# Loading a ranked expert's gate and up matrix in one 2 MB transfer instead of two of 1 MB

## The chip, the cores and the metric

The kernel runs on one core of a Trainium2 chip. The metric is the device time of one execution in microseconds, the median of the runs. The core's engines work side by side, each through its own list of instructions: TensorE (PE) multiplies, VectorE (DVE), ScalarE (ACT) and GpSimd (POOL) do the rest, and SyncE (SP) issues nearly all transfers from memory (HBM) to the on-chip memory (SBUF). Semaphores hold an instruction until what it needs is there.

## The reference

One layer of a decoder trunk for 256 tokens of width 1024 in float32: an adaptive norm, a mixer (convolution module and differential attention, gated and summed), and a second adaptive norm with a mixture of 64 small experts, of which each token uses 8, and a shared expert. The change lies in the experts:

```python
g, u = jnp.split(jnp.einsum('td,edf->tef', tc, w_gu), 2, axis=-1)
return jnp.einsum('tef,efd->td', jax.nn.silu(g) * u * gc[..., None], w_down)
```

`w_gu` of one expert is 1024 x 512 (2 MB) and `w_down` 256 x 1024 (1 MB), so the experts bring 192 MB of weights through the core's transfers.

## The kernel before

**Blocks.** After routing, the kernel orders the experts by how many tokens chose them, and packs their tokens into blocks of 128 rows. Blocks 0 to 2 hold six experts known beforehand (numbers 0 to 5), blocks 3 to 27 the 58 ranked ones. The string `PAT` (L36) gives the kinds of blocks 3 to 27: `Q` packs four experts of 32 rows, `P` two of 64, `M` one of 96 and one of 32, `H` one of 128. The numbers of the experts of a kind run on, so block 3 (Q) holds 44 to 47, block 4 (P) 14 and 15, block 5 (Q) 48 to 51, block 6 (Q) 52 to 55, block 7 (P) 16 and 17, block 8 (Q) 56 to 59, block 9 (P) 18 and 19, block 10 (P) 20 and 21; block 25 (Q) holds 60 to 63, block 26 (P) 34 and 35, block 27 (P) 36 and 37.

**Work of one block on PE** (`experts`, L1799): the gate and up product, eight k steps with one matmul for each expert in every step (L1811, called GU below); the combination of the block before (L1719); two transposes (L1836); half the gather of a later pair of blocks (L1528) and two small steps (L1569, L1572); the down product (L1862, called D). Then the next block's GU. The last block's down product is `finale` (L1744, L1756). The shared expert's matmuls (L1793, L1634, L1656) are put between them.

**Weights.** They come through one list of loads in a fixed order, L306 to L346: for a block, the first half of the gate and up matrix (k steps 0 to 3) of each of its experts, then the second halves, then the down matrices. Each load is 1 MB and goes to a landing place of 8 KB in each of the 128 partitions. From block 3 on 14 places are handed out again and again, named by their offset in KB: 0, 8, 16, 24, 32, 40, 96, 104, 112, 120, 128 and 136 in the tile `fa`, 144 and 152 in `late_w`. `advance` (L361) gives the next load of the list the place that has been free longest, and `load` (L384) issues it with `dma` (L269) on SP's queue. `done` (L435) frees a place: a first half's when GU has done k step 3, a second half's after k step 7, a down matrix's after D. In blocks 0 and 1 a place is handed on by halves (`halves`, L359): after two k steps its first half takes half of the next load, 512 KB. SP waits for the place's last reader before it issues a transfer, and also for the transfer eight before it, since eight semaphores are used in turn.

**Order.** A planner (`Plan`, L49) runs while the program is built: every piece of work is a coroutine with an estimated cost, and the planner's clock decides in which order the instructions are written and which place each load gets. At run time that order is fixed.

Of the kernel before, what the change touches and what calls it, by code (L numbers as in the profile page):

```python
# [18 lines left out]
KB = 256  # L19
# [20 lines left out]
class Event:  # L40
    t = None
# [159 lines left out]
def tile_hybrid_block(ctx, tc, x, c, positions, w_ada, b_ada, norm1_g, w_in, conv_dw, conv_dw_b,  # L201
# [21 lines left out]
    late_w = []  # L223
    B = [ps.tile([P, 512], F32, name=f"bank{i}") for i in range(8)]

    def fa(kb, n):
        return FA[:, int(kb * KB):int(kb * KB) + n]
# [41 lines left out]
    def dma(o, i):  # L269
        return nc.sync.dma_start(o, i)  # L270
# [51 lines left out]
    blocks = [("P", [i, i + 1]) for i in range(0, NS, 2)]  # L322
    for kd in pat:
        js = []
# [14 lines left out]
    for b in [1, 0, 2, *range(3, len(blocks))]:  # L339
        js = blocks[b][1]  # L340
        gs = [("g", j, q) for q in range(2) for j in js]
        ds = [("d", j, 0) for j in js]
        if b == len(blocks) - 1:
            ds = [("d", j, 0, cs) for cs in ENDS for j in js]
            gs = [("g", j, q, c_) for q in range(2) for c_ in range(2) for j in js]
        order += gs + ds  # L346
# [3 lines left out]
    loaded = {}  # L350
    todo = list(order)
    eid, idi = {}, []
# [5 lines left out]
    halves, LAST = {}, 160  # L358
    w2s = ExitStack()  # L359

    def advance(now, half=None):  # L361
        pool = pl.pools["w"]
        while todo:
            kind, i, q, *cut = todo[0]
            more = cut and cut[0] in (1, *ENDS[1:])
            if not pool and not more and half is None:
                return
            w = loaded.setdefault((kind, i), Weights())
            if kind in ("g", "d") and i >= NS and not idi:
                return  # L370
            todo.pop(0)
            if not more:
                pool.sort(key=lambda e: e[0])
                w.slot, off = pool.pop(0) if half is None else (now, half)
                if not q:
                    w.k, w.at, w.off = [None] * 16, [0.0] * 16, []
                w.off.append(off)
            if half is not None:
                halves[half] = kind, i, q
                load(kind, i, q, [0], now)  # L380
                return
            load(kind, i, q, cut, now)

    def load(kind, i, q, cut, now):  # L384
        w = loaded[kind, i]
        off = w.off[q]
        if kind in ("g", "d"):
            wsrc = w_exp_gu if kind == "g" else w_exp_down
            if i < NS:
                wsrc = wsrc[0, i]  # L390
            else:
                if i not in eid:
                    eid[i] = nc.sync.value_load(idi[0][0:1, i:i + 1], min_val=0, max_val=NE - 1)
                wsrc = wsrc[0, bass.ds(eid[i], 1)].rearrange("o a b -> (o a) b")
        elif kind in ("sg", "sd"):
            wsrc = (w_sh_gu if kind == "sg" else w_sh_down)[0]
        elif kind == "b":
            wsrc = w_ada[0][:, q * D + i * 256:q * D + (i + 1) * 256]
        else:
            wsrc = src[kind][i]  # L400
        nk = {"d": 2, "sd": 2, "b": 8}.get(kind, 4)
        t = fa(off, 2048) if off < 144 else late_w[0][:, (off - 144) * KB:(off - 136) * KB] if off < LAST else late_w[1]
        t = t.rearrange("p (k n) -> p k n", k=nk)
        wsrc = wsrc.rearrange("(p k) n -> p k n" if kind in ("g", "d", "sg", "sd") else "(k p) n -> p k n", p=P)
        if kind != "b":
            wsrc = wsrc[:, q * nk:(q + 1) * nk]
        cuts = 2 if cut else 1
        st = max(dma_free[0], max(w.slot, now) + 2.0)
        size = (2.48 if kind in ("g", "d", "sg", "sd") else 2.92) / max(cuts, 1)
        if cut and cut[0] in ENDS:  # L410
            dma(t[:, :, cut[0]], wsrc[:, :, cut[0]])
            st += 2.48 * (cut[0].stop - cut[0].start) / D
            w.k[0:2] = t[:, 0], t[:, 1]
            pl.ev("Ld", i, cut[0].start).t = 0.0
            w.ends = {**getattr(w, "ends", {}), cut[0].start: st + ARRIVE}
            cut = []
            cuts = 0
        for c_ in cut or range(cuts):
            ks = slice(c_ * nk // cuts, (c_ + 1) * nk // cuts)
            dma(t[:, ks], wsrc[:, ks])  # L420
            st += size
            for k in range(ks.start, ks.stop):
                w.at[q * nk + k] = st + ARRIVE
                w.k[q * nk + k] = t[:, k]
                pl.ev("L", kind, i, (q * nk + k) // 2).t = 0.0
        dma_free[0] = st
        if q and params and kind != "b" and not cut and cuts:
            n, prm = params.pop(0)
            dma(*prm)
            pl.ev("param", n).t = st + ARRIVE  # L430

    def done(key, q, now=None):
        now = pl.cur.ready if now is None else now
        w = loaded[key]
        if w.off[q] in halves:  # L435
            e = halves.pop(w.off[q])
            load(*e, [1], now)
            advance(now)
        elif w.off[q] in once:
            once.remove(w.off[q])  # L440
        elif w.off[q] == LAST:
            w2s.close()
            obs = ctx.enter_context(tc.tile_pool(name="obs", bufs=1)).tile([P, 8 * KB], F32R, name="obs")
            pl.put("ob", *(ob_of(obs[:, i * D:(i + 1) * D]) for i in range(2)))
        else:
            pl.pools["w"].append((now, w.off[q]))
            advance(now)

    advance(0.0)


# [887 lines left out]
    key = late([NE, NE + 1])  # L1339
# [624 lines left out]
    with tc.If(novf > 0):  # L1964
        wg = fa(0, 4096).rearrange("p (k n) -> p k n", k=K)
        wd = fa(16, 2 * D).rearrange("p (k n) -> p k n", k=2)
        gcol, sg, act, aT = fa(88, 2), fa(89, 256), fa(90, 256), fa(91, 256).rearrange("p (f s) -> p f s", f=2)
        with tc.For_i(0, novf, 1) as i:
# [5 lines left out]
            for t in range(2):  # L1974
# [9 lines left out]
                for h in range(2):  # L1984
                    d = slice(h * 512, (h + 1) * 512)
# [31 lines left out]
```

## Time and profile before

| | us |
|---|---|
| median of 3 runs (820.06 to 821.34) | 820.31 |
| the profiled execution | 821.83 |
| its span in the trace | 820.0 |
| PE busy in the span | 768.2 (94%) |
| DVE, ACT, POOL busy | 444.6, 325.5, 192.0 |

The transfers moved 271 MB, of which 192 MB are the experts'. The page's strip has 40 slices of 20.5 us, and a digit is the busy share in tenths; for the transfers it is the mean share of 16 DMA engines. The timeline lists one engine's instructions, neighbours of a kind merged: start, length, line, count, and in brackets the idle time ahead of it and what ended that. A float32 matmul stands there as two instructions, so the GU of a P block is x32, that of a Q block x64. Where experts' places lie in two tiles, the rows of one k step are split in two.

### The profile page before, as it was taken

The numbers are of one execution on the slowest core, as the hardware profiler recorded it, in microseconds if no ns is written. First come the engines' busy times: TensorE is split into PE (matmuls) and PEld (weight loads), VectorE is DVE, ScalarE is ACT, GpSimd is POOL, SyncE is SP. The second block draws the span as 40 slices with busy tenths as digits, with TensorE's granted clock in tenths as the row PEclk, the third lists the DMA queues.
The fourth block names the chain that finished last, engine by engine and source line by source line (L and its number), as shares of the span: only waits on it lengthen the run. The fifth ranks groups of instructions, "written<-read, shape, count | busy, mean of one in ns | idle before, by whom it ended". The sixth has DMA issues, their size and how long they took to land.

```text
span 820.0 us, 13174 instructions
## 1 busy us (share of the span) xinstructions
PE 768.2 (94%) x4759; PEld 473.9 (58%) x4759; DVE 444.6 (54%) x1035; ACT 325.5 (40%) x714; POOL 192.0 (23%) x246
## 2 busy tenths in 40 slices
PE   3999999899996999999999697899999999999997
PEld 2898777589793987745454152354464455454543
DVE  5458988979996677543433041344344344433343
ACT  4357656864758864323222021233232232232220
POOL 3003888778573683100001000000000000000000
PEclk9999989889998999999999899999999999999999
DMA  9998766537554586389999999999999999999993
GB/s 319 364 344 279 263 248 219 194 116 256 206 194 166 179 302 231 133 328 362 404 420 420 422 421 420 420 422 421 420 421 420 421 422 420 420 421 418 419 412 132
DMA packets 69883, 271.04 MB, mean 331 GB/s; under 512 B 6085, under 2 KB 15893, under 8 KB 46520
## 3 DMA queue, kind: packets, MB, share of 16 engines
q1 hardware_dynamic: 69464, 270.00, 84.4%
q8 instruction: 38, 0.62, 0.3%
q0 software_dynamic: 304, 0.16, 0.1%
q14 instruction: 29, 0.24, 0.1%
q10 hardware_dynamic: 48, 0.01, 0.0%
HBM read 269.11 MB, written 1.05 MB: 329 GB/s over the span
## 4 chain that ended last, share of the span: by engine, by line


## 5 line engine op out<-in xcount | busy, mean ns | idle before, releaser
L1811 PE MATMUL bank<-fa 128*32 128x512 f32 (+2 forms) x1048 | 203.1, 600 | 11.3 <-DMA fa<-in_w_exp_gu_dram 11.3
L1811 PEld LDWEIGHTS bank<-fa 128*32 128x32 f32 (+2 forms) x1048 | 60.9, 123 | 133.3 <-issue 108.0
L863 DVE SCALAR_TENSOR_TENSOR bank<-fa,tap,bank 128x256 f32<-128x256 f32 x232 | 113.0, 487 | 6.1
L1685 DVE SCALAR_TENSOR_TENSOR fa<-bank,gsc,h 128x256 f32<-128x256 f32 x28 | 13.6, 484 | 170.9 <-ACT h L1681 170.9
L1862 PE MATMUL bank<-fa 128*32 128x512 f32 (+1 forms) x496 | 84.9, 596 | 0.8 <-DMA fa<-in_w_exp_down_dram 0.7
L1681 ACT ACTIVATE h<-bank 128x256 f32<-128x256 f32 x28 | 10.8, 385 | 187.9 <-PE bank L1811 187.9
L776 POOL TENSOR_TENSOR rb<-fa,rb 128x512 fp32r<-128x512 f32 x46 | 60.1, 1314 | 65.8 <-ACT rb L795 63.9
L1703 DVE TENSOR_TENSOR fa<-bank,fa 128x512 f32<-128x512 f32 x54 | 37.4, 692 | 65.2 <-PE bank L1862 65.0
L776 POOL TENSOR_TENSOR ra<-fa,ra 128x512 fp32r<-128x512 f32 x48 | 63.8, 1335 | 25.6 <-ACT ra L795 22.2
L1728 DVE TENSOR_TENSOR fa<-fa,bank 128x512 f32<-128x512 f32 x108 | 66.9, 681 | 0.0
L1771 ACT CAST obs<-fa 128x512 fp32r<-128x512 f32 x54 | 33.4, 619 | 82.6 <-DVE fa L1703 82.6
L795 ACT CAST ra<-fa 128x512 fp32r<-128x512 f32 x76 | 46.8, 622 | 40.9 <-PE bank L812 24.6
L1528 PE MATMUL bank<-ra 128*128 128x256 f32 x448 | 60.7, 288 | 0.0
L1496 ACT ACTIVATE fa<-bank,b2c,a2c 128x256 f32<-128x256 f32 x108 | 53.6, 561 | 17.7 <-PE bank L1528 16.7
L1719 PE MATMUL bank<-obs,ra 128*128 128x512 f32 x216 | 58.9, 413 | 0.0
L795 ACT CAST rb<-fa 128x512 fp32r<-128x512 f32 x68 | 42.0, 624 | 37.4 <-PE bank L812 22.4
L1528 PEld LDWEIGHTS bank<-ra 128*128 128x128 f32 x448 | 55.6, 191 | 0.2
L1811 PE MATMUL bank<-late_w,fa 128*32 128x512 f32 (+2 forms) x168 | 51.5, 628 | 4.1 <-DMA late_w<-in_w_exp_gu_dram 4.1
L1719 PEld LDWEIGHTS bank<-obs,ra 128*128 128x128 f32 x216 | 38.5, 188 | 29.1 <-issue 21.9
L811 PE MATMUL bank<-ra 128*128 128x256 f32 x160 | 48.5, 303 | 1.9 <-ACT ra L577 1.8
L1862 PEld LDWEIGHTS bank<-fa 128*32 128x32 f32 (+1 forms) x496 | 22.9, 119 | 42.7 <-issue 34.8
L812 PE MATMUL bank<-ra 128*128 128x256 f32 x160 | 46.7, 292 | 0.1
(377 smaller groups left out, 1399.3 us busy)
## 6 DMA issues: line engine op xcount, KB each, us to landing
fa<-in_w_exp_gu_dram SPq DMA_DIRECT2D x100, 1024.0 KB, 19.7
fa<-in_w_exp_down_dram SPq DMA_DIRECT2D x50, 1024.0 KB, 19.8
fa<-in_w_ada_dram SPq DMA_DIRECT2D x24, 1024.0 KB, 7.9
fa<-in_w_in_dram SPq DMA_DIRECT2D x22, 1024.0 KB, 5.3
late_w<-in_w_exp_gu_dram SPq DMA_DIRECT2D x17, 1024.0 KB, 19.7
late_w<-in_w_exp_down_dram SPq DMA_DIRECT2D x12, 1024.0 KB, 7.9
fa<-in_w_exp_gu_dram SPq DMA_DIRECT2D x22, 512.0 KB, 9.2
fa<-in_w_in_dram SPq DMA_DIRECT2D x12, 512.0 KB, 9.3
```

The source lines that it names most:

```text
L776: (nc.gpsimd if e == "G" else nc.vector).tensor_tensor(hl[:, 1], w.k[k], hl[:, 0].bitcast(F32), op=OP.subtract)
L795: nc.scalar.copy(hl[:, 0], w.k[k])
L811: nc.tensor.matmul(o, hl[:, 0, mm], src_t[:, k, 0], start=(k == 0 and m % 2 == 0), stop=False)
L812: nc.tensor.matmul(o, hl[:, 0, mm], src_t[:, k, 1], start=False, stop=False)
L863: nc.vector.scalar_tensor_tensor(cv[:, m] if j == TAPS - 1 else acc, u_sb[:, m, j:j + T], tap[:, m, j:j + 1], acc, op0=OP.mult, op1=OP.add)
L1496: nc.scalar.activation(xt[:, k, 0:ns], p3[:, f2, 0:ns], AF.Identity, bias=b2c[:, k:k + 1], scale=a2c[:, k:k + 1])
L1528: nc.tensor.matmul(p3[:, f2, 0:ns], xr[:, a, t, (f + f2) * P:(f + f2 + 1) * P], tables[b0][:, t, 0:ns], start=(f2 + t + a == 0), stop=(f2 ...
L1703: nc.vector.tensor_tensor(o32, pd[h], g2b[:, h * 512:(h + 1) * 512], op=OP.mult)
L1719: nc.tensor.matmul(p, info.pT[:, t * P:(t + 1) * P], ob[a], start=(a == 0), stop=(a == 1))
L1728: nc.vector.tensor_tensor(x_sb[:, t, d], x_sb[:, t, d], p, op=OP.add)
L1811: nc.tensor.matmul(pg[o:o + m], info.xt[:, k, o:o + m], loaded["g", js[e]].k[k], start=(k == 0), stop=(k == K - 1))
L1862: nc.tensor.matmul(pd[h][o:o + m], info.aT[:, f, o:o + m], loaded["d", js[e]].k[f][:, h * 512:(h + 1) * 512], start=(f == 0), stop=(f == 1))
```

## The change

For blocks 3 to 26 (56 experts) the two loads of an expert's gate and up matrix become one of kind `G`: 2 MB, in each partition one run of 16 KB instead of two of 8 KB. It lands in two neighbouring places, an offset that 16 divides and the next one. So the 14 places form seven pairs. `advance` takes the pair whose later half was freed first, and returns with nothing issued when no pair is free; loads behind it in the list wait too. A `G` is not started in half a place. A down matrix takes one place, by preference one whose neighbour is not free. Freeing stays as it was. Blocks 0 to 2 and 27 load as before.

```diff
+        if 2 < b < len(blocks) - 1:
+            gs = [("G", j, 0) for j in js]
...
+            if kind == "G":
+                at = {off: t for t, off in pool}
+                pairs = [(max(at[off], at[off + 8]), off) for off in at if off % 16 == 0 and off + 8 in at]
+                if half is not None or not pairs or not idi:
+                    return
+                todo.pop(0)
+                w = loaded.setdefault(("g", i), Weights())
+                w.slot, off = min(pairs)
+                w.k, w.at, w.off = [None] * 16, [0.0] * 16, [off, off + 8]
+                pool[:] = [e for e in pool if e[1] not in w.off]
+                load("g", i, 0, [], now, True)
+                continue
...
-                pool.sort(key=lambda e: e[0])
+                free = {off for _, off in pool}
+                pool.sort(key=lambda e: (bool(idi) and e[1] ^ 8 in free, e[0]))
...
-    def load(kind, i, q, cut, now):
+    def load(kind, i, q, cut, now, both=False):
...
-        nk = {"d": 2, "sd": 2, "b": 8}.get(kind, 4)
+        nk = 8 if both else {"d": 2, "sd": 2, "b": 8}.get(kind, 4)
...
-        size = (2.48 if kind in ("g", "d", "sg", "sd") else 2.92) / max(cuts, 1)
+        size = 4.84 if both else (2.48 if kind in ("g", "d", "sg", "sd") else 2.92) / max(cuts, 1)
```

The places that the changed program hands out, where the prediction speaks of them, and what lay there:

| transfer | places | read last by |
|---|---|---|
| G of 44 | 112, 120 | expert 3 of block 1, k steps 3 and 7 |
| G of 45 | 96, 104 | expert 2 of block 1, k step 7; expert 4 of block 2, k step 3 |
| G of 14, 15 | 112, 120; 96, 104 | G of 44, G of 45 (block 3) |
| G of 52 | 144, 152 | G of 48 (block 5) |
| G of 18 | 96, 104 | G of 56 (block 8) |
| G of 34, 35 | 16, 24; 112, 120 | G of 60, G of 61 (block 25) |

On SP, at the first ranked experts, the kernel before has these rows (the TENSOR_LOAD reads an expert's number, a row 128x1024 is half a load, 128x2048 a load of 1 MB):

```order
L270 DMA fa<-in_w_exp_gu_dram 128x1024
L393 TENSOR_LOAD ids
L393 ISA x2
L270 ISA
L270 DMA fa<-in_w_exp_gu_dram 128x1024
L270 ISA
L270 DMA fa<-in_w_exp_gu_dram 128x1024
L270 ISA
L270 DMA fa<-in_w_exp_gu_dram 128x1024
L270 ISA
L270 DMA fa<-in_w_exp_gu_dram 128x2048
```

In the changed program the same place has these, with 128x4096 for 2 MB and line numbers 15 higher behind the edit:

```order
L408 TENSOR_LOAD ids
L408 ISA x2
L270 ISA
L270 DMA fa<-in_w_exp_gu_dram 128x4096
L408 TENSOR_LOAD ids
L408 ISA x2
L1978 TENSOR_LOAD olist
L1978 ISA x2
L270 ISA
L270 DMA fa<-in_w_exp_gu_dram 128x4096
```

Eight transfers of 512 KB and four of 1 MB became four of 2 MB; the read of `olist` (the list of experts with too many tokens), which stood near the program's end, now stands between the first and the second.

On PE, behind block 3's down product, the kernel before runs block 4's GU, with the shared expert's matmul (L1793) in its middle, then the combination, and most of the shared expert behind block 4:

```order
L1811 MATMUL bank_73<-fa 64x512 x8
L1793 MATMUL bank_79<-fa 128x256
L1811 MATMUL bank_73<-fa 64x512 x8
L1719 MATMUL bank_74<-obs,ra 128x512 x2
L1719 MATMUL bank_78<-obs,ra 128x512 x2
```

The changed program has at this place (L1808, L1649, L1671 are the shared expert's three lines, L1826 is GU, L1734 the combination):

```order
L1808 MATMUL bank_79<-fa 128x256 x4
L1649 MATMUL bank_76<-ident,fa 128x128 x2
L1671 MATMUL bank_74<-fa 128x512 x2
L1649 MATMUL bank_79<-ident,fa 128x128 x2
L1671 MATMUL bank_78<-fa 128x512 x2
L1826 MATMUL bank_73<-fa 64x512 x16
L1734 MATMUL bank_77<-obs,ra 128x512 x2
L1734 MATMUL bank_76<-obs,ra 128x512 x2
```

Two thirds of the shared expert moved ahead of block 4's GU; from block 6 on the order of the kinds of work on PE is as before.

## Rows read from the trace of the kernel before

**Rows 1.** The page's strip: busy tenths of the transfers, and GB/s.
```profile
DMA  9998766537554586389999999999999999999993
GB/s 319 364 344 279 263 248 219 194 116 256 206 194 166 179 302 231 133 328 362 404 420 420 422 421 420 420 422 421 420 421 420 421 422 420 420 421 418 419 412 132
```

**Rows 2.** By stretch: length, busy of PE, PEld, DVE, ACT, POOL; clock, DMA share, GB/s.
```profile
464.70:471.50 6.80, 6.02 (x26) 1.34 (x26) 0.00 (x0) 0.00 (x0) 0.00 (x0) 0.50 1.01 420
...
541.80:590.00 48.20, 48.20 (x298) 22.95 (x296) 21.29 (x49) 13.96 (x29) 0.00 (x0) 1.00 1.01 421
```

**Rows 3.** PE's waits from 427 to 541.8 us: total, times, longest.
```profile
PE bank L1811 <- DMA fa<-in_w_exp_gu_dram: 11.3, 10, 1.5
PE bank L1811 <- DMA late_w<-in_w_exp_gu_dram: 4.1, 3, 1.5
```

**Rows 4.** SP's waits, the longest of 400 to 600 us, then of 690 to 800.
```profile
SPq L270 <- DMA fa<-in_w_exp_gu_dram: 76.5, 44, 2.1
...
SPq L270 <- PE bank L1862: 39.9, 6, 7.1
```

**Rows 5.** Transfers by kind: count, KB each, median us to landing.
```profile
fa<-in_w_exp_gu_dram SPq DMA_DIRECT2D x100, 1024.0 KB, 19.7
...
fa<-in_w_sh_down_dram SPq DMA_DIRECT2D x1, 1024.0 KB, 4.7
```

**Rows 6.** A stretch with transfers in runs of 2 KB (columns as in Rows 2).
```profile
70.00:75.00 5.00, 5.00 (x44) 5.00 (x44) 4.33 (x10) 3.70 (x6) 2.58 (x2) 1.00 1.03 390
```

**Rows 7.** PE's timeline: GU of blocks 1, 2 and 3.
```profile
357.01 7.04 PE L1811 MATMUL bank<-fa 128*64 128x512 f32 x32
...
374.73 1.03 PE L1811 MATMUL bank<-fa 128*64 128x512 f32 x4
...
376.02 6.23 PE L1811 MATMUL bank<-fa 128*64 128x512 f32 x28
...
391.17 7.07 PE L1811 MATMUL bank<-fa 128*32 128x512 f32 x64
```

**Rows 8.** PE's timeline: D of blocks 5, 6, 7; GU of 7, 10.
```profile
445.75 3.64 PE L1862 MATMUL bank<-fa 128*32 128x512 f32 x32
...
476.65 3.64 PE L1862 MATMUL bank<-fa 128*32 128x512 f32 x32
480.22 4.51 PE L1811 MATMUL bank<-fa 128*64 128x512 f32 x18
485.37 3.65 PE L1811 MATMUL bank<-fa 128*64 128x512 f32 x14 [0.65 <-DMA fa<-in_w_exp_gu_dram]
...
493.58 3.65 PE L1862 MATMUL bank<-fa 128*64 128x512 f32 x16
...
541.79 7.04 PE L1811 MATMUL bank<-fa 128*64 128x512 f32 x32
```

**Rows 9.** PE's timeline: one block without waits, from D to D.
```profile
583.68 3.64 PE L1862 MATMUL bank<-fa 128*32 128x512 f32 x32
587.25 7.09 PE L1811 MATMUL bank<-fa 128*64 128x512 f32 x32
...
598.89 3.65 PE L1862 MATMUL bank<-fa 128*64 128x512 f32 x16
```

**Rows 10.** PE's timeline: block 6's GU, two k steps at the lower clock.
```profile
466.34 1.07 PE L1811 MATMUL bank<-fa 128*32 128x512 f32 x2
...
467.19 1.07 PE L1811 MATMUL bank<-fa 128*32 128x512 f32 x2
```

**Rows 11.** PE's timeline: GU of blocks 25 and 26, and the finale.
```profile
768.97 7.07 PE L1811 MATMUL bank<-fa 128*32 128x512 f32 x64
...
784.17 0.64 PE L1811 MATMUL bank<-fa 128*64 128x512 f32 x1
...
807.29 3.66 PE L1744 MATMUL bank<-fa 128*64 128x512 f32 x24 [0.46 <-ACT fa L1694]
```

More of the change, by code (lines that the diff above doesn't have):

```diff
@@ L400, in load @@
             wsrc = src[kind][i]
-        nk = {"d": 2, "sd": 2, "b": 8}.get(kind, 4)
-        t = fa(off, 2048) if off < 144 else late_w[0][:, (off - 144) * KB:(off - 136) * KB] if off < LAST else late_w[1]
+        nk = 8 if both else {"d": 2, "sd": 2, "b": 8}.get(kind, 4)
+        t = fa(off, 4096) if both and off < 144 else late_w[0] if both else fa(off, 2048) if off < 144 else late_w[0][:, (off - 144) * KB:(off - 136) * KB] if off < LAST else late_w[1]
         t = t.rearrange("p (k n) -> p k n", k=nk)
```

## The prediction

> **What bounds the kernel now.** I read the strip first: from slice 20 to the end but one the transfers are fully busy and move 420 GB/s [rows 1]. So from 400 to 800 us the stream of weights is a limit, 1 MB every 1.0486/0.421 = 2.49 us. Next the busy time by stretch: from 541.8 us on PE shows no idle time either [rows 2], and its clock is full. PE's waits lie ahead of that: between 427 and 541.8 us it waits for gate and up matrices 11.3 + 4.1 us, in pieces of 1.5 us at most [rows 3]. The reader is to see two limits that hand over: up to 541.8 us PE works each matrix off as it lands, and behind that PE is the limit, one block in 598.89 - 583.68 = 15.2 us [rows 9], while the weights of a two-expert block take 6 x 2.49 = 14.9 us. What block 10's GU loses in its start at 541.79 [rows 8] is lost to the end, unless PE gets less to do, and it does not.
>
> Next SP's waits: up to 600 us SP mostly waits for the transfer eight before [rows 4], so a transfer is issued 19.7 us ahead of its landing [rows 5]; late in the kernel, from 690 us on, it waits for PE to free a place instead [rows 4]. The places are sufficient now, without much to spare.
>
> **What the change saves.** Runs of 2 KB move at 390 GB/s [rows 6], runs of 8 KB at 421 [rows 2]: 2.69 against 2.49 us for 1 MB, with 512 runs against 128. So a run costs 0.20/384 = 0.52 ns on top of its bytes. A 2 MB matrix in 128 runs rather than 256 saves 0.067 us, 4.98 down to 4.91 us; for 56 experts 3.7 us of stream. The bounds are 0 (if nothing is saved above 8 KB) and twice that; I take 0.07. PE gets none of it directly: its matmuls, and those of every other engine, are the same ones. SP issues 56 transfers fewer, which costs and brings nothing, since it waits anyway [rows 4].
>
> **What it costs: whole matrices.** PE today starts on first halves while the second are under way: block 7's GU starts at 480.22, stops after 18 of 32 instructions and goes on at 485.37 [rows 8]. Afterwards it needs the whole 2 MB of every expert of the block. The Trainium skill says the same of one transfer (DMA: Bandwidth & Descriptors, "Why a DMA increments its semaphore by 16 and not by 1"): only the full count means that the data has landed, and a smaller one does not tell which bytes have. By it no k step can start on a part of the 2 MB, and a wait for the last matrix of a Q block has a whole GU behind it.
>
> **What it costs: pairs.** A pair is free only when both its places are, so a 2 MB transfer starts later than two single ones, and what stands behind it waits too. I walk the stream by hand, with four numbers: 4.7 - 2.49 = 2.2 us from issue to the first byte, from the one lone 1 MB transfer of the experts' kind [rows 5]; 4.91 us for a G, 2.49 us for a down matrix; and on PE 598.89 - 587.25 = 11.6 us from a GU's start to its D, of which GU is 7.1 [rows 9].
>
> Block 1's GU ends at 364.05 [rows 7], which frees the pair of expert 44: landed at 364.05 + 2.2 + 4.91 = 371.2. The pair of 45 needs k step 3 of block 2, of whose 32 instructions 4 stand from 374.73 and 28 from 376.02 [rows 7]: the 16th ends near 378.4. So 45 lands at 385.5, the queue stands empty for 9.4 us, and 46 and 47 land at 390.4 and 395.3. Before, half places let eight transfers of 512 KB go out in this time. (`olist`, which SP now reads ahead of 45, is written from matmuls of block 1's time, ten us earlier; the wait for the pair covers it.) Block 3's GU starts at 395.3, not 391.17 [rows 7].
>
> From there the stream runs on: the down matrices land by 405.3, and the pair of 14, freed at 395.3 + 7.1 = 402.4, can bring bytes at 404.6, with 0.7 us to spare. 14 and 15 land by 415.1, their down matrices by 420.1, 48 to 51 by 439.7, their down matrices by 449.7. Block 5's GU starts at 439.7, its D at 451.3; before 445.75 [rows 8]. The shared expert's matmuls that moved ahead of block 4 fill part of the wait there. The pair of 52 is free at 446.8, bytes from 449.0, again 0.7 us to spare; 55 lands at 469.3, block 6's D starts at 480.9 (476.65 before). 16 and 17 land by 489.1, block 7's D starts at 500.7 (493.58 before). 59 lands at 513.7; the pair of 18, freed at 520.8, has 0.6 us to spare. 19 lands at 533.4, block 9's D starts at 545.0, and block 10's GU 3.6 us later, at 548.6 instead of 541.79: **6.8 us**.
>
> In this walk PE waits 4.1, 7.9, 14.4, 4.6, 9.4 and 4.5 us in front of six GUs, in one piece each. Before, a run of waits of 1.5 us was enough for the granted clock to be 0.50 (1.2 GHz) for 6.8 us [rows 2]; a k step took 467.19 - 466.34 = 0.85 us there [rows 10] instead of 7.04/16 = 0.44. A full such stretch costs 3.4 us of work. Three of the six waits (ahead of blocks 3, 5 and 8) stand in front of a pair with 0.6 or 0.7 us to spare, so a slow GU passes up to 2.7 us on to the stream, 8 us for three; the lower bound is 0. I take **3.5 us**, because half of the waits are long. A third part is the stream between 375 and 400 us: the strip shows 362 and 404 GB/s there [rows 1], and the same walk for the kernel before brings block 5's weights 2.6 us too early. I take **1 us** of 0 to 2.6.
>
> From block 10 to 25 PE is the limit as before, 15 blocks of 15.2 us = 228 us, if the stream keeps ahead. It has 12 blocks of 14.8, two of 7.4 and 60 to 63's 19.6 us to bring: 212 us. The pairs take away 10.5 us more, by the same walk: 3.4 in front of 42, 5.3 of 13, and four times under 1. So it arrives some 5 us early, and the shift stays.
>
> At block 25 it grows again. The pairs of 34 and 35 are those of 60 and 61, free when block 25's GU ends (768.97 + 7.07 = 776.0 before [rows 11]; call it T). 35 lands at T + 2.2 + 9.8 = T + 12.0. Block 26's GU started at T + 8.2 without waiting (784.17 [rows 11]); now it waits **3.8 us**. Block 27 loads as before; its last halves land at T + 27.2, during its GU, and its last down pieces at T + 32.3, while the finale, at T + 31.3 before [rows 11], is at T + 35.1. So these 3.8 us go to the end. A fall of the clock in that wait adds 0 to 3.4; I take **0.7**.
>
> The sum: 6.8 + 3.5 + 1 + 3.8 + 0.7 = 15.8 us. Against the profiled execution that is 821.8 + 15.8 = 837.6; the median lies 1.5 us below that execution, so I predict **836 us**, 1.9% slower.
>
> **Rivals.** *The clock stays up* (12 in 100): 6.8 + 3.8 = 10.6 us at most, less 1.7 if G's come faster by the upper bound, so 829 to 831. Against it: one wait of 14.4 us where 1.5 us pieces were enough. *The clock falls every time* (20 in 100): 6.8 + 8 + 2.6 + 3.8 + 3.4 = 24.6 us, 845. *The early loss is absorbed* (5 in 100): PE's 16 us of waits [rows 3] swallow the 9.4 us, and only the tail is lost, 824. It needs the stream ahead of PE by 541 us, and there it runs without a stop already. *Nothing waits for a pair, so it is faster* (5 in 100): the planner's pairs come free in time, the queue never runs empty, and the 24 experts up to block 10 bring 24 x 0.067 = 1.6 us, which PE, the limit from there on, keeps: 818.7. It decides on 45: were its pair free by 369, the early hole would close. Rows 7 put it at 378.4. *16 KB runs are cut in two on the way*, so that no time is saved: 1.6 us more than my sum, 838, inside my forecast. *Each merged transfer saves a fixed cost*: with eight transfers under way, 1 MB every 2.49 us against 4.7 for a lone one [rows 5] leaves none of it to save. The Trainium skill gives a fixed 2 us for a transfer (DMA: Bandwidth & Descriptors, "Anatomy of one DMA"); the trace hides it. Were it paid, 24 transfers fewer by block 10 would end PE's waits [rows 3], 16 us, and give 804; I put 1 in 100 of the 5 there.
>
> **How the numbers follow.** Forecast 832 to 840: 55 in 100. Clock always down, 840 to 846: 20. Clock up, 827 to 832: 12. Absorbed, 822 to 827: 5. No change: 3. Faster: 5. I leave out the last three with a little above 845, and give 827 to 845. A measurement of this kernel tells 0.2% (1.6 us) from no change; faster 0.05, same 0.03, slower 0.92.
>
> **What would show it.** In the changed kernel's profile: the strip of transfers with a hole of some 9 us near 371 to 380 us; block 3's GU at 395, block 10's near 553; PE's waits for gate and up matrices in few long pieces, some 40 us rather than 15; a clock of 0.50 in two or three stretches between 395 and 540 us; a wait of about 4 us in front of block 26's GU; 2 MB transfers back to back every 4.91 us. I am wrong if 45 lands before 380 us, if PE waits no more than before, or if the transfers show no hole.

## The result

The changed kernel takes 844.5 us (median of four runs, 844.2 to 847.4), the kernel before beside it 820.2. The ratio on record is 1.0312 (95% interval 1.0287 to 1.0337), or 25.6 us; the two medians by themselves lie 24.3 us apart. The forecast was 836 us with a range up to 845. The direction held, and in the main the mechanism. The size did not: about 25 us where the sum had 15.8, at or just beyond the upper end of the range.

The profiled execution of the changed kernel ("after" below) has a span of 845.6 us against 820.0, 25.6 us more; the accounts below are of these two executions. From their pages: the busy line of PE (share, instructions), first of before, then of after; then after's strip, which answers to [rows 1].

```profile
PE 768.2 (94%) x4759; PEld 473.9 (58%) x4759; DVE 444.6 (54%) x1035; ACT 325.5 (40%) x714; POOL 192.0 (23%) x246
```
```profile
PE 777.3 (92%) x4759; PEld 473.5 (56%) x4759; DVE 445.1 (53%) x1035; ACT 325.5 (38%) x714; POOL 191.9 (23%) x246
...
PEclk9999999799997999998999798899999999999989
...
GB/s 313 364 341 280 261 214 251 199 152 199 199 212 157 209 319 170 202 191 419 370 424 423 426 425 388 413 424 427 424 427 363 395 423 376 322 397 423 400 406 90
```

The same 4,759 matmul instructions keep PE busy 9.1 us longer: some 8 us of that is a slower clock, 1.2 us a GU that stood still in its middle (block 25, below). The other 25.6 - 9.1 = 16.5 us are idle time. The transfers, closed in [rows 1] from slice 20 nearly to the end (the first slice is number 0), now have holes: slice 17 (191 GB/s), 19 (370), 24 (388), and many from slice 30 on. Where nothing stops them they move 424 to 427 GB/s rather than 420 to 422.

PE's waits of after from 390 us to the end (total, times, longest), which answer to [rows 3], and SP's from 360 to 400 us:

```profile
PE bank L1826 <- DMA fa<-in_w_exp_gu_dram: 30.9, 11, 3.9
PE bank L1826 <- DMA late_w<-in_w_exp_gu_dram: 2.2, 1, 2.2
```
```profile
SPq L270 <- PE bank L1826: 15.6, 3, 10.0
```

So PE waits 33.1 us for gate and up matrices where it was 15.4, a difference of 17.7, about the idle time found above. SP, which in [rows 4] waited for transfers, now stands 10.0 us in one wait for a matmul: the pair of expert 45. By stretch (columns as in [rows 2]) the hole behind that wait, the handover, and the stage in which PE is the limit:

```profile
365.00:375.00 10.00, 10.00 (x66) 6.57 (x65) 4.84 (x17) 5.21 (x11) 0.00 (x0) 1.00 0.46 187
375.00:385.00 10.00, 10.00 (x49) 4.69 (x48) 4.07 (x9) 1.41 (x4) 0.00 (x0) 1.00 0.57 204
...
440.00:541.00 101.00, 77.00 (x465) 30.53 (x461) 27.43 (x58) 18.19 (x38) 0.00 (x0) 0.87 0.99 414
541.00:785.00 244.00, 244.00 (x1484) 119.02 (x1486) 95.78 (x211) 66.61 (x142) 0.00 (x0) 0.99 0.97 401
```

PE's timeline of after, GU of blocks 3, 9 and 10, of 25, 26 and the finale (start, length, idle time ahead and its end); compare [rows 7, 8, 11]:

```profile
391.73 1.60 PE L1826 MATMUL bank<-fa 128*32 128x512 f32 x6
397.20 9.63 PE L1826 MATMUL bank<-fa 128*32 128x512 f32 x58 [3.87 <-DMA fa<-in_w_exp_gu_dram]
...
541.00 9.44 PE L1826 MATMUL bank<-fa 128*64 128x512 f32 x30 [3.83 <-DMA fa<-in_w_exp_gu_dram]
...
558.50 1.89 PE L1826 MATMUL bank<-fa 128*64 128x512 f32 x8
...
785.67 8.26 PE L1826 MATMUL bank<-fa 128*32 128x512 f32 x64
...
803.52 1.07 PE L1826 MATMUL bank<-fa 128*64 128x512 f32 x2 [1.39 <-DMA fa<-in_w_exp_gu_dram]
808.41 8.86 PE L1826 MATMUL bank<-fa 128*64 128x512 f32 x30 [3.82 <-DMA fa<-in_w_exp_gu_dram]
...
833.32 1.94 PE L1759 MATMUL bank<-fa 128*64 128x512 f32 x8 [0.46 <-ACT fa L1709]
```

Block 10's GU starts at 558.50 instead of 541.79, 16.7 us late. From there to block 25's GU it takes 227.2 us in both kernels. Behind it the shift grows to 833.32 - 807.29 = 26.0 us at the finale. Block 25's GU takes 8.26 instead of 7.07 us [rows 11] at a granted clock of 1.00; in it the weight loads (PEld) stand once, behind the first k step of three of its four experts:

```profile
786.87 0.16 PEld L1826 LDWEIGHTS bank<-fa 128*32 128x32 f32 x8 [1.05 <-DMA fa<-in_w_exp_gu_dram]
```

The loss thus has two parts, 16.7 us up to block 10 and 9.3 us at blocks 25 and 26.

### The profile page after: what moved, and what is told of

It reads as the page before. It is cut to its first block, busy times and chain, and to the rows that moved or that the text cites. A ratio compares the mean times of both kernels' runs of the same rounds, so it can differ in the third digit from the quotient of the medians.

```text
span 845.6 us, 12878 instructions
## 1 busy us (share of the span) xinstructions
PE 777.3 (92%) x4759; PEld 473.5 (56%) x4759; DVE 445.1 (53%) x1035; ACT 325.5 (38%) x714; POOL 191.9 (23%) x246
## 3 DMA queue, kind: packets, MB, share of 16 engines
HBM read 269.11 MB, written 1.05 MB: 319 GB/s over the span
## 4 chain that ended last, share of the span: by engine, by line
## 5 line engine op out<-in xcount | busy, mean ns | idle before, releaser
L1826 PE MATMUL bank<-fa 128*32 128x512 f32 (+2 forms) x1048 | 222.1, 630 | 31.0 <-DMA fa<-in_w_exp_gu_dram 30.9
L1826 PEld LDWEIGHTS bank<-fa 128*32 128x32 f32 (+2 forms) x1048 | 63.8, 128 | 163.7 <-issue 118.9
L1877 PE MATMUL bank<-fa 128*32 128x512 f32 (+2 forms) x512 | 91.0, 596 | 0.0
L1826 PE MATMUL bank<-late_w,fa 128*64 128x512 f32 (+1 forms) x168 | 78.2, 618 | 2.2 <-DMA late_w<-in_w_exp_gu_dram 2.2
L810 ACT CAST ra<-fa 128x512 fp32r<-128x512 f32 x76 | 46.8, 622 | 39.7 <-PE bank L827 24.3
L1734 PE MATMUL bank<-obs,ra 128*128 128x512 f32 x216 | 58.9, 413 | 0.0
L1734 PEld LDWEIGHTS bank<-obs,ra 128*128 128x128 f32 x216 | 38.5, 188 | 28.7 <-issue 21.5
L1877 PEld LDWEIGHTS bank<-fa 128*32 128x32 f32 (+2 forms) x512 | 25.6, 122 | 47.8 <-issue 40.8
## 6 DMA issues: line engine op xcount, KB each, us to landing
late_w<-in_w_exp_gu_dram SPq DMA_DIRECT2D x10, 2048.0 KB, 11.6
```

What stands on the lines that cost most here:

```text
L810: nc.scalar.copy(hl[:, 0], w.k[k])
L1734: nc.tensor.matmul(p, info.pT[:, t * P:(t + 1) * P], ob[a], start=(a == 0), stop=(a == 1))
L1826: nc.tensor.matmul(pg[o:o + m], info.xt[:, k, o:o + m], loaded["g", js[e]].k[k], start=(k == 0), stop=(k == K - 1))
L1877: nc.tensor.matmul(pd[h][o:o + m], info.aT[:, f, o:o + m], loaded["d", js[e]].k[f][:, h * 512:(h + 1) * 512], start=(f == 0), stop=(f == 1))
```

## The experiments

The profiled executions differ in the part ahead of block 2, which the change leaves as it is: its GU starts at 369.0 to 374.7 us. Besides the ratio on record I therefore give, from PE's timeline of each profiled execution, the time from block 2's GU to block 10's D (**early**) and from there to the end of the span (**late**); the kernel before has 553.39 - 374.73 = 178.7 and 820.04 - 553.39 = 266.7, the changed kernel 570.10 - 374.22 = 195.9 and 845.63 - 570.10 = 275.5. The last two columns are the differences to the kernel before.

| run | median us | ratio (95%) | early | late |
|---|---|---|---|---|
| changed kernel | 844.5 | 1.0312 (1.0287 to 1.0337) | +17.2 | +8.9 |
| e1_early | 836.6 | 1.0195 (1.0151 to 1.0239) | +16.6 | 0.0 |
| e2_late | 833.9 | 1.0191 (1.0120 to 1.0261) | +5.4 | +10.2 |
| e3_middle | 826.4 | 1.0092 (1.0060 to 1.0124) | +5.1 | +2.1 |
| e4_places | 820.1 | 1.0004 (0.9982 to 1.0026) | +0.6 | -0.2 |
| e5_split | 828.1 | 1.0119 (1.0074 to 1.0164) | +6.9 | +1.0 |
| e6_filler | 835.4 | 1.0208 (1.0176 to 1.0240) | +9.4 | +4.4 |
| e7_b3old | 836.7 | 1.0211 (1.0180 to 1.0241) | +10.9 | +8.8 |
| e8_swapped | 844.3 | 1.0313 (1.0282 to 1.0343) | +17.3 | +7.6 |
| e9_land | 842.3 | 1.0282 (1.0236 to 1.0327) | +18.2 | +6.1 |
| e10_wait | 840.3 | 1.0254 (1.0208 to 1.0299) | +15.5 | +6.0 |
| e11_bfill | 818.7 | 0.9991 (0.9965 to 1.0016) | +0.5 | -0.3 |

**Where: the change on some of the blocks alone.**

```diff
-        if 2 < b < len(blocks) - 1:
+        if 2 < b < 10:                  (e1_early)
+        if 9 < b < len(blocks) - 1:     (e2_late)
+        if 9 < b < 25:                  (e3_middle)
+        if 3 < b < len(blocks) - 1:     (e7_b3old)
```

> The merged 2 MB transfers only for blocks 3 to 9 (24 experts); blocks 10 to 26 load in two halves as the kernel before. Theory 'pairs': all that was lost by block 10's GU (558.50 against 541.79 us, 16.7) is lost here too, and nothing behind it: block 10 at 558 us, block 26's GU without a wait, 820 + 17 = 837 us. Rival 'the loss at the end is caused by the slow start and would come anyway' (the stream never catches up): 844 us as the changed kernel. Rival 'the loss of the start is made up when single places come back': under 830 us.

> The merged transfers only for blocks 10 to 26 (32 experts); blocks 3 to 9 as before. Theory 'pairs': block 10's GU at 542 us as before, PE the limit up to block 25, then the wait for the pairs of experts 60 and 61 in front of block 26 and a slow GU behind it: 4 to 9 us, so 824 to 829 us. Rival 'runs of 16 KB bring time where pairs come free in time': 816 to 819 us. Rival 'the late part is harmless unless the stream is already behind': 820 us.

> Whole matrices by pairs only for blocks 10 to 24, where PE is the limit; blocks 3 to 9, 25 and 26 as in the kernel before. Theory that the loss lies before block 10 and at block 26 alone: 820 to 822 us, ratio 1.000 to 1.003, with block 10's D to the end as long as before (266.6 us), plus at most the 5 us that the run with blocks 10 to 26 lost ahead of block 10. Theory that pairs also slow the middle: 826 us or more, with PE waiting for gate and up matrices behind 560 us. Theory that longer runs are worth their saved stream time: below 818 us.

> The changed kernel with block 3 (experts 44 to 47) loaded as before, in halves and quarters; all later blocks up to 26 as changed. Theory that the empty queue in front of expert 45 starts the loss and is handed on: the hole near 367 to 375 us goes, block 10's GU moves by 6 to 10 us rather than 16.7, 834 to 839 us. Theory that the first hole is absorbed or made up by later ones (pairs of 14, 52, 18): 842 to 846 us. If the first hole is all of the early loss: 829 to 830 us.

Blocks 3 to 9 alone cost 16.6 us, all of it early, as expected. Blocks 10 to 26 alone cost more than I expected (833.9 for 824 to 829): besides the tail, some 5 us at block 10, although its weights come behind an undisturbed stream. The run with blocks 10 to 24 shows why, in PE's timeline of block 10's GU:

```profile
539.51 1.02 PE L1826 MATMUL bank<-fa 128*64 128x512 f32 x2
542.62 8.78 PE L1826 MATMUL bank<-fa 128*64 128x512 f32 x30 [2.08 <-DMA fa<-in_w_exp_gu_dram]
```

Before, this GU ran through in 7.04 us [rows 8], on the first halves of 20 and 21 while the last half was still coming. Now nearly all of it stands behind the whole of 21, and it runs 8.78 instead of 7.1 us, since the granted clock is 0.50 from 543.6 to 547.0 us. Four of the eight k steps more behind the last byte are 3.5 us, the clock 1.7: together about the 5.1 us measured, by arithmetic. The early losses of this run and of e1_early (5.1 and 16.6) do not add up in the changed kernel (17.2): there block 9 is so late that block 10's matrices have landed, and its GU runs through in 7.04 us. The run with blocks 10 to 24 also loses 2.1 us late, though blocks 25 and 26 load as before: its stream falls behind in the middle, and PE waits 1.2 us in block 26's GU, where the kernel before has no wait.

The run without block 3 is the test of the hole in front of 45. The hole goes (its strip has 351 GB/s in slice 17), and so do 6.3 of the 17.2 early us; the other 10.9 stay. So the first hole is about a third of the early loss, and the later pairs make the rest.

**What: the places, the split, and the two things that a joined transfer joins.**

```diff
-        if 2 < b < len(blocks) - 1:
+        if False:                       (e4_places: only the new choice of places is left)
...
-            dma(t[:, ks], wsrc[:, ks])
+            for hs in ((slice(0, 4), slice(4, 8)) if both else (ks,)):                 (e5_split)
+            for hs in ((slice(4, 8), slice(0, 4)) if both else (ks,)):                 (e8_swapped)
+            for hs in ((slice(7, 8), slice(0, 4), slice(4, 7)) if both else (ks,)):    (e10_wait)
+                dma(t[:, hs], wsrc[:, hs])
...
+                for j in js if not k and (2 < b < 11 or 24 < b < len(blocks) - 1) else ():      (e9_land, on top of e5_split)
+                    nc.tensor.matmul(pg[:, 0:32], ident, loaded["g", j].k[7][:, 0:32], start=True, stop=True)
```

> Only the new preference of single loads for a place whose neighbour is not free; all matrices in two transfers of 1 MB as before. Every theory that puts the loss on the pairs or on the 2 MB transfers expects 820 us, within 0.3%. If which place a load gets were itself the cause (a place that is read later), some of the 24 us would show here.

> The changed kernel with the same order, the same places and the same pairs, but each pair filled by two transfers of 1 MB (runs of 8 KB) one behind the other, so that PE can begin with a first half. Theory 'pairs' (the transfer starts late because both places must be free): the hole of 9 us in the stream near 375 us stays, the waits shrink by the half transfer (2.5 us) in front of a GU and by the quicker start of an empty queue (4.7 against 9.05 us for 2 MB): block 10 at 552 to 556 us, 835 to 841 us in all. Rival 'whole matrices' (the loss is that PE waits for 2 MB and that 2 MB start slowly): 822 to 828 us. Rival 'run length' (16 KB runs are themselves worth something): slower than the changed kernel, 847 us.

> Order and places of the changed kernel; each 2 MB matrix goes out as two 1 MB transfers, its second half first. The transfer to the place that comes free last so stands in front, and PE, which starts on the first half, needs both: the joint wait and the joint landing stay, the size of a transfer and its runs of 8 KB are those of before. With the first half in front it took 828 us. Theory that the joint wait and the joint landing make the loss: 840 to 846 us. Theory that the slow start of a 2 MB transfer on an empty queue (9 us from issue to landing) is a part of it: 2 to 5 us less than the changed kernel, 838 to 842. Theory that the size of the transfer is all: 826 to 830 us, as with the first half in front.

> Order and places of the changed kernel, each matrix as two 1 MB transfers, first half in front (as in the run that took 828 us), but ahead of its first k step a block multiplies 32 columns of the last k step's rows of each of its matrices by a unit matrix, so that it starts only when the matrices have landed whole (blocks 3 to 10, 25 and 26). Each half still waits for its own place alone: this is the joint landing without the joint wait. Theory that the joint wait in front of the transfer makes the larger part of the 16 us between the split and the joined transfer: 828 to 833 us. Theory that the joint landing makes the larger part: 838 to 844 us. Shares alike: 834 to 838 us. The small matmuls themselves add at most 2 us where they don't lie in a wait.

> Order and places of the changed kernel; each matrix as three transfers: first the last of its eight k steps (256 KB, in the place that comes free last), then the first half, then the other three k steps. So the first half, like the rest, waits for both places, while PE starts as soon as the first half has landed: the joint wait without the joint landing. Theory that the joint wait makes the larger part of the 16 us: 838 to 844 us. Theory that the joint landing does: 828 to 833 us. Shares alike: 834 to 838 us. With three transfers for a matrix the eight under way hold fewer bytes; that could add 1 to 2 us.

The new choice of places alone costs nothing. With the order and the pairs of the changed kernel but two transfers for each matrix, e5_split loses 9.8 us by its ratio and not 25.6. Each half there waits for its own place and lands by itself. The 6.9 us that it still loses early are close to what the first hole cost above: SP issues the first half of 45 at 359.5 us and the second, whose place is read in block 2, at 373.1 (in this run's time), and slice 17 of its strip, below, has 267 GB/s. That this hole is all of the rest is not shown. Turning the two halves round, e8_swapped, brings back the whole loss, 844.3 us, with transfers of 1 MB in runs of 8 KB and 56 transfers more: neither the size of a transfer, nor its run, nor the number of transfers, nor how late a 2 MB transfer lands on an empty queue (last section) decides. What the swap adds is that the transfer in front waits for the place that comes free last, and that PE, which begins on the first half, begins only when both are there.

I expected e9_land (joint landing alone) and e10_wait (joint wait alone) to share the 16 us between them, or one to carry them. Neither came: each alone costs nearly all of it, 842 and 840 us, by the ratios 23.1 and 20.8 us where both together cost 25.6 and neither 9.8. Both runs are a little harsher than the bare wait: in e9_land a block does not even begin the first k steps before its last matrix is there, and in e10_wait the stream mostly moves 412 to 418 GB/s where nothing stops it, against 420 to 422, which may be 1 to 2 us up to block 10 (an estimate from these rates). The strips of e5_split, e9_land and e10_wait, in this order:

```profile
GB/s 318 365 347 288 264 230 230 216 157 220 216 181 150 234 309 204 193 267 311 422 420 420 421 421 421 422 421 421 419 422 421 420 420 422 357 389 421 417 415 175
```
```profile
GB/s 317 365 361 281 247 251 217 201 210 145 202 256 143 228 274 201 208 238 405 383 349 421 422 421 416 398 421 421 420 422 420 408 421 386 314 395 423 393 410 101
```
```profile
GB/s 318 364 343 278 268 222 248 201 170 182 201 220 159 207 316 170 199 192 393 368 416 412 421 414 418 379 418 418 415 417 417 417 415 417 340 389 415 417 412 142
```

From slice 19 up to block 10's start, in slice 26, the split stream stands at 420 to 422 and never stops. In both others it stops again and again (383 and 349; 368, then 379). This is a loop: a place comes free, its transfer goes out, lands, PE works it off, the place comes free. The prediction's walk gave that loop 0.6 to 0.7 us to spare at the pairs of 14, 52 and 18. Landing together holds a GU back by up to a half's 2.49 us, waiting together holds a transfer back by half a GU, 3.5 us. Each is more than what was to spare, so each alone opens the holes, and the second adds little. That reading fits all five runs (the changed kernel and these four); but the spare time was worked out, not measured, so why the two do not add is argued, not shown.

**The clock.** Filler matmuls (128x512, 0.87 us each) in the waits ahead of some GUs, in the changed kernel and in the kernel before; transfers and places stay.

```diff
+            for _ in range({3: 5, 6: 11, 8: 5, 9: 4, 26: 5}.get(b, 0)):      (e6_filler, changed kernel)
+            for _ in range({5: 3, 6: 11, 7: 3, 8: 5, 9: 3}.get(b, 0)):       (e11_bfill, kernel before)
+                nc.tensor.matmul(pg, ident, wr.rearrange("p k n -> p (k n)"), start=True, stop=True)
```

> The changed kernel with 30 idle-filling matmuls (128x512, float32, into a bank that the block's GU overwrites afterwards) set in front of the GUs of blocks 3, 6, 8, 9 and 26, in the waits that stand there; transfers, places and their order are those of the changed kernel. It tells what the falls of PE's clock cost. Theory that the clock's falls are a part of the loss: the clock of 0.50 behind those waits goes away, GU 3, 8, 9 and 26 run at their full-clock length of about 7.1 us rather than 8.9 to 11, pairs come free earlier, 836 to 840 us. Theory that the waits for the 2 MB matrices alone set the time: 844 to 846 us, since what the filler saves is waited for at the next matrix anyway. If the filler itself delays the GUs it would be over 846.

> The kernel before with the same filler matmuls in front of the GUs of blocks 5, 6, 7, 8 and 9 (3, 11, 3, 5 and 3 of them), so that the one stretch of half clock at 465 to 471 us goes away; nothing else is changed. Theory that a fall of the clock costs only where a transfer waits for the place that the slow GU holds: in the kernel before the stream runs on without a stop there, so nothing is gained, 818 to 820 us. Theory that such a fall costs its 3.4 us wherever it stands: 815 to 817 us.

In the changed kernel they give back 9.1 us by the medians (844.5 to 835.4) and 8.5 by the ratios. Between the profiled executions it is 7.8 early and 4.5 late, 12.3 in all; that of the filled kernel lies 4.5 us below its median. Its granted clock over the whole span is 0.981, the highest of the four runs (the others have 0.973 to 0.977), so in those a fall may have stayed. The clock line of its page, and PE's remaining waits:

```profile
PEclk9999999799997999999999999999999999999999
```
```profile
PE bank L1828 <- DMA fa<-in_w_exp_gu_dram: 8.6, 3, 3.8
PE bank L1828 <- DMA late_w<-in_w_exp_gu_dram: 2.2, 1, 2.2
```

The waits are shorter here because the filler fills them and counts as work; that the end comes some 9 us earlier is the clock's part. In the kernel before, the same filler takes away the only slow stretch of this time, which had 0.50 in [rows 2]:

```profile
464.70:471.50 6.80, 6.80 (x52) 3.70 (x44) 2.37 (x5) 0.76 (x2) 0.00 (x0) 1.00 1.01 418
```

and the time stays (0.9991, 0.9965 to 1.0016; 3.4 us less would have been 0.9959). So in these two kernels a fall of the clock cost nothing where the stream ran on beside it, and some 9 us where transfers waited for the places that the slow GUs held.

## Why the prediction was right in sign and short in size

**The step that failed is the clock's term.** The sum had 3.5 + 0.7 = 4.2 us for it. The filler, which takes the falls of the clock away and leaves places and order, gives back 8.5 to 9.1 us, and 12.3 between the two profiled executions. The walk kept PE at full clock throughout and put the clock in afterwards as a lump; but a slow GU hands its delay on through the next pair. I had that reason in hand, with an upper bound of 8 us ahead of block 10, and took less than half of it, with a clock of 0.50 "in two or three stretches" up to 540 us where there are five up to 546. A smaller slip, measured against its term, is in the waits. The sum without the clock had 6.8 + 1 + 3.8 = 11.6 us; the filled run still loses 9.4 + 4.4 = 13.8 us in its profiled execution, in which no fall is left, and 17.0 by its ratio. Step by step:

- **Two limits that hand over at 541 us: right.** From block 10 to block 25 the shift stays (227.2 us in both), and blocks 3 to 9 alone give the early loss.
- **What longer runs save: right, and worth nothing here.** GU pieces that begin as a 2 MB transfer lands lie 4.90 and 4.91 us apart (463.88, 468.78 and 473.69 us), as worked out. The swapped run, with runs of 8 KB, takes as long as the changed kernel (1.0313 and 1.0312).
- **Whole matrices and pairs: the right mechanism**, and the transfer of 45 went out when forecast (378.34 us; the walk had 378.4). But the walk was short at every station: block 5's D at 455.68 (walk 451.3), 6's at 487.19 (480.9), 7's at 507.38 (500.7), block 10's GU at 558.50 (548.6). Besides the clock, the landing of 45 was mis-sized: 9.1 us after its issue, not 7.1.
- **The rival whose clock falls every time, 845 us, came closest**, in the time and in its clock terms: 8 + 3.4 = 11.4 us.
- **The slow k step was misnamed.** The 0.44 us that the prediction calls a k step is half of one (eight k steps make a GU of 7.04 us); the ratio of the two clocks, which it uses, is not touched by that.
- **The arrival "some 5 us early" at block 25: wrong.** Block 25's GU stood 1.05 us for a matrix that was still coming, its fourth, and the run with blocks 10 to 24 lost 2.1 us behind block 10. The pairs' 10.5 us in the middle were about right: that run's strip has 371, 404, 389 and 313 GB/s in slices 31 to 34, and (4 x 421 - 1477)/421 x 20.6 = 10.1 us of stream are missing. What the stream had ahead was less.
- **Block 26: the wait was forecast as 3.8 us and came as 1.39 + 3.82**, and the GU behind it then runs 8.86 instead of 7.1 us. With block 25's 1.2 us the tail costs 9.3, not 4.5.
- **The waits' form: wrong.** I gave six waits of up to 14.4 us in one piece; there are twelve, none over 3.9, because PE does the first k step of each expert as it lands. Their sum, 33 us, was forecast as some 40.

The other rivals fall. The early loss was not absorbed: 16.7 us are still there at block 10. The clock did not stay up. And no fixed cost of a transfer came back: the swapped run issues 56 transfers more than the changed kernel and takes as long. The section that the prediction names for such a cost in the Trainium skill (DMA: Bandwidth & Descriptors, "Anatomy of one DMA") describes transfers issued from GpSimd, while SP issues these.

## What to carry to other kernels

Joining two transfers joins two waits: the one for the places and the one for the data. Before joining, look at the loop from place to transfer to work to place and at what it has to spare. Here that was some 0.6 us by the walk, less than half a transfer, and the longer run was bought with holes in the stream. And where PE waits inside such a loop, walk it with the slow clock in it from the start, rather than adding the clock at the end.

## What the runs showed of the hardware

A 2 MB transfer that goes out on an empty queue lands later than its own bytes need. Expert 45's in after (count, KB, us from issue to landing), and the stretch from its issue to its landing (columns as in [rows 2]):

```profile
fa<-in_w_exp_gu_dram SPq DMA_DIRECT2D x1, 2048.0 KB, 9.1
```
```profile
378.30:387.40 9.10, 9.10 (x54) 5.60 (x50) 3.37 (x9) 2.34 (x6) 0.00 (x0) 1.00 0.88 336
```

In these 9.1 us 336 x 9.1 = 3.06 MB moved, although 45 is 2.1 MB: about a third belongs to transfers issued behind it, the next one 1.2 us after it. At 424 GB/s, the lower of the rates above, 3.06 MB take 7.2 us, so the first bytes came no later than the 2.2 us of [rows 5] suggest (an estimate). The transfers under way thus share the engines, and those behind take bytes before the first has landed; the walk had them one after the other. Another transfer of 2 MB, issued at 641.21 us with the next one again 1.2 us behind it, took 8.5 us. The swapped run shows that this doesn't set the time here.

In after the granted clock was 0.50, the level of 1.2 GHz, at 395.6 to 402.4 us, 463.9 to 477.5, 494.6 to 498.0, 515.1 to 521.9, 539.0 to 545.8 and 805.2 to 812.0. At each of these falls PE was in a wait of 3.7 to 3.9 us for weights, at the end of one, or had just left one of 2.2 us. A wait of 2.11 us ahead of 444.06 us brought no fall, while in the run with blocks 10 to 24 the clock fell behind one of 2.08.
